# Two rows of activations as one 512-column operand in the SwiGLU output products and the mixer's output projection

## The chip, the cores and the metric

One core of a Trainium2 chip runs the whole program as one launch. The metric is the device time of that launch in microseconds (us), the median of the runs shown; less is better. PE is TensorE's matmuls, PEld its weight loads, DVE VectorE, ACT ScalarE, POOL GpSimd, SP the queue that issues the DMAs.

## The reference, cut to what matters

A two-layer encoder trunk over 256 positions of 1024 channels. Each layer has three sub-layers: a SwiGLU block, three token mixers with a merged output projection, and a second SwiGLU block; each ends in a residual and a LayerNorm:

```python
def swiglu(h, wi, wo):
    gu = h @ wi                                   # (256, 1024) @ (1024, 5632)
    return (jax.nn.silu(gu[..., :D_FF]) * gu[..., D_FF:]) @ wo   # (256, 2816) @ (2816, 1024)
...
x = layer_norm(ALPHA * x + 0.5 * mod[:, :, 2] * swiglu(h, ...), ln_w[l, 0], ln_b[l, 0])
...
x = layer_norm(ALPHA * x + mod[:, :, 5] * (merged @ w_out), ln_w[l, 1], ln_b[l, 1])
```

All of it is float32. The modulation `mod` is a product of the condition vector with a large matrix (`ada_w`), different for each sub-layer.

## The kernel before

Activations stand transposed: 128 channels on the partitions, 256 positions along a row, so a 1024-channel activation is 8 tiles of 128x256 and the 2816-channel one of a SwiGLU block is 22. A weight block is 128x128 and is the stationary operand; a product of one output tile m accumulates over its k blocks in one PSUM bank.

To keep float32's precision with the one-pass type float32r, most products are taken in three parts. `unit` (L321) loads up to 1024 columns of weights by one DMA into `raw` (4 buffers) and splits them in pieces of 512 columns, four k blocks each: `whi` is ACT's rounded copy, `wlo` DVE's remainder (5 buffers each). Activations are split in the same way by `split` (L308): `hhi`/`hlo` for the modulated input (`h_split`, L450), `ahi`/`alo` for the SwiGLU's product (L658 to 661), `hhi`/`hlo` again for the merged mixer output (L1364 to 1367). `mm3` (L341) then issues three matmuls per k block, of 128x128 weights by 256 columns each: `whi` by the high part, `whi` by the low part, `wlo` by the high part. All three add into the same 256 columns of a bank (`dense`, L349; `dbank`, L255, takes the first 256 of a bank's 512 columns, with 4 buffers). The mixers' input projections use `plain` float32 weights and an unsplit `h` instead (`h_split` with plain=True).

A SwiGLU block (`ffn`, L624) has two stages. In the first, 22 pairs of output tiles run over 8 k blocks. In the second (L663 to 669), 8 output tiles m run over 22 k blocks in three units of 8, 8 and 6; these are the second SwiGLU products. `side_work` (L373) puts pieces of the modulation (`ada`, L416: a DMA of 512 KB and a 1.22 us pass on DVE each) between the units. After each m, `ln_put` (L536) takes the bank: one DVE pass makes the residual `r = psum * gate + xa` (L541), then ACT squares it, DVE adds it into two running sums, and ACT (and DVE) prepare it as operand of the first products of the next sub-layer. For m = 0 a small matmul makes a mean that is taken off first. After m = 7 four matmuls make the LayerNorm's statistics; `early` (L510) issues the first four products of the next sub-layer, so that PE has work while `ln_end` (L570) finishes the norm.

The mixers end (L1432 to 1440) in the output projection: 8 output tiles over 8 k blocks with `wout`, each again followed by `ln_put`.

The order of instructions within an engine is laid by the Tile framework's scheduler, which may interleave what the source has one after the other; each engine then works its own list in order and waits on semaphores.

Of the kernel before, what the change touches and what calls it, by code (L numbers as in the profile page):

```python
# [10 lines left out]
F32R = mybir.dt.float32r  # L14
AF = mybir.ActivationFunctionType
# [4 lines left out]
MUL, ADD, SUB, MAX, MIN = ALU.mult, ALU.add, ALU.subtract, ALU.max, ALU.min  # L20

D, L, DEPTH, FF = 1024, 256, 2, 2816
NT, NF = D // 128, FF // 128
# [188 lines left out]
class Builder:  # L212
# [136 lines left out]
    def dense(self, out, w, x, off=0, k0=0, nk=8, first=True, last=True):  # L349
        for k in range(nk):  # L350
            self.product(out, w, off + k * 128, x[k0 + k], first and k == 0, last and k == nk - 1)

    def product(self, out, w, off, x, first, last, cols=128):
        if isinstance(w, list):
            self.mm3(out, w, off, x, first, last)
        else:
            self.mm(out, w[:, off:off + cols], x, first, last)
# [90 lines left out]


    def h_split(self, m, src, a, b, on_act=False, plain=False):  # L450
        h = self.t("hhi", 256, 8) if plain else self.t("hf", 256, 2)
        if on_act:
            x = self.act(h[:], src, AF.Identity, scale=a, bias=b)
        else:
            x = self.ts(h[:], src, a, MUL, b, ADD)
        if plain:
            self.h[m] = h[:]
            return x, x, x
        hi = self.t("hhi", 256, 8, F32R)
        lo = self.t("hlo", 256, 8, F32R)  # L460
        self.h[m] = (hi[:], lo[:])
        return (x, *self.split(hi[:], lo[:], h[:]))

    def start(self):
        x = self.x0 = self.lt("xa", (8, 256))
# [67 lines left out]
            self.ready[key] = y, wab[:, 1:2]  # L533
        self.adv = []

    def ln_put(self, m, psum):  # L536
        l, sub = self.lsub
        mod = self.mods[(l, sub)]
        r, xa = self.r, self.xa
        assert (l, sub, 2) in self.done  # L540
        self.stt(r[:, m, :], psum, mod[:, 16 + m:17 + m], xa[:, m, :], MUL, ADD)  # L541
        if m == 0:
            pb = self.bank("s", 2)
            self.mm(pb[:, 0:256], self.ones, r[:, 0, :], True, True)
            sm = self.sm = self.lt("lsm")
            self.act(sm[:], pb[:, 0:256], AF.Copy, scale=1.0 / 128)

            self.tt(xa[:, 1, :], xa[:, 1, :], sm[:], SUB)
            self.tt(r[:, 0, :], r[:, 0, :], sm[:], SUB)
            self.s1, self.s2 = self.lt("racc"), self.lt("lsa")  # L550
            self.act(self.s2[:], r[:, 0, :], AF.Square)
            self.u_put(0)
            return
        sq = self.lt("lsq", bufs=2)
        self.act(sq[:], r[:, m, :], AF.Square)
        if m < 7:
            x = self.tt(self.s1[:], r[:, 0, :] if m == 1 else self.s1[:], r[:, m, :], ADD)
            self.after(self.tt(xa[:, m + 1, :], xa[:, m + 1, :], self.sm[:], SUB), x)
            self.tt(self.s2[:], self.s2[:], sq[:], ADD)
        self.u_put(m)  # L560
        if m == 6:
            self.act(self.warm[:], sq[:, 0:1], AF.Ln, bias=1.0)
            self.p1, self.p2 = self.bank("s", 2), self.bank("s", 2)
            self.mm(self.p1[:, 0:256], self.onesd[:], self.s1[:], True, False)
            self.mm(self.p2[:, 0:256], self.onesd[:], self.s2[:], True, False)
        if m == 7:
            self.mm(self.p1[:, 0:256], self.onesd[:], r[:, m, :], False, True)
            self.mm(self.p2[:, 0:256], self.onesd[:], sq[:], False, True)
# [55 lines left out]
    def ffn(self, l, i):  # L624
        sub = 2 * i
        ap = self.ap
        acts = []
# [4 lines left out]
        for j in range(NF):  # L632
            ps, ws = [], []
            for q in (0, 1):
# [3 lines left out]
                else:  # L638
                    w = self.unit(u)
# [13 lines left out]
            pr = self.pt("ada_raw", 1024, 3)[:, 0:256]  # L653
            if ws or not pair:
                self.tt(pr, sg[:], pu, MUL)
            else:
                self.stt(pr, pu, bu, sg[:], ADD, MUL)
            hi = self.pt("ahi", 256, NF, F32R)  # L658
            lo = self.pt("alo", 256, NF, F32R)
            self.split(hi[:], lo[:], pr)  # L660
            acts.append((hi[:], lo[:]))
        self.ln_begin(l, sub)
        for m in range(8):  # L663
            pd = self.dbank()
            for k0, nk in ((0, 8), (8, 8), (16, 6)):
                self.side_work(m == (0 if own else SIDEM) and k0 == 0)
                w = self.unit(ap["wo"][l, i, m, :, k0:k0 + nk, :].rearrange("p k c -> p (k c)"), nk * 128)
                self.dense(pd, w, acts, 0, k0, nk, k0 == 0, k0 == 16)
            self.ln_put(m, pd)
        if sub == 0:  # L670
            self.early(self.mix_units(l)[:NE], NE)
        elif l + 1 < DEPTH:
# [676 lines left out]
    def merge(self, l, br, ys, first, last):  # L1349
        mg = self.mg  # L1350
        for m in range(8):
            gs = self.pt("gi", 256, 3)
            self.dma(gs[:], self.gd[br][:, m, :])
            if m % 2 == 0:
                w = self.unit(self.ap["pab"][l, br, m // 2].rearrange("p m k c -> p (m k c)"))
# [5 lines left out]
                self.stt(gs[:], gs[:], 1.0, pp, ADD, MUL)  # L1361
                self.tt(mg[:, m, :], mg[:, m, :], gs[:], ADD)
            if last:
                hi = self.t("hhi", 256, 8, F32R)  # L1364
                lo = self.t("hlo", 256, 8, F32R)
                self.split(hi[:], lo[:], mg[:, m, :])
                self.mh.append((hi[:], lo[:]))

    def mixers(self, l):
        A = self.A  # L1370
# [24 lines left out]
        with self.phase("w") as self.wp, self.phase("l") as self.lp:  # L1395
# [36 lines left out]
            self.relief = REL[5]  # L1432
            for m in range(8):
                w = ws[m] if m < NPRE else self.unit(wout[m])
                pd = self.dbank()
                self.dense(pd, w, self.mh)
                self.ln_put(m, pd)
            self.early(self.ffn_units(l, 1)[:NE], NPRE)
            self.relief = 0
            self.ln_end()  # L1440
# [53 lines left out]
```

## Time and profile before

| | before |
|---|---|
| median of 3 runs (lowest to highest) | 1677.54 us (1676.74 to 1681.32) |
| the profiled execution's own time | 1676.47 us |
| its span in the trace | 1674.7 us |
| PE busy, weight loads busy | 1583.2 us (95%), 1432.8 us (86%) |
| DVE, ACT, POOL busy | 1154.3, 804.9, 274.4 us |
| moved by DMA | 355.75 MB, mean 212 GB/s |

How to read it: matmuls are pipelined, so a record's duration (some 280 ns for a 256-column float32r matmul) is longer than the distance at which the next one starts; the distance is found by dividing a stretch by the matmuls in it. A weight load has a record of its own (LDWEIGHTS). "f32" in a shape also stands for float32r operands of PE.

### The profile page before, as it was taken

Reading aid. Unit: us, or ns where it says so; the run is one execution under the profiler, and the core shown is the slowest. Engines: PE = TensorE matmul, PEld = TensorE weight load, DVE = VectorE, ACT = ScalarE, POOL = GpSimd, SP = SyncE. Lnnn points to the kernel's source line nnn. Section 1 sums busy time; section 2 is a strip of 40 time slices with the busy share of each in tenths; the row PEclk is TensorE's granted clock in tenths of the full one; section 3 lists DMA queues with packets and bytes.
Section 4 is the critical chain, followed back from the end, with each engine's and each line's share of the span. In section 5 each row is a group of like instructions: output and inputs, shape, how many; then the busy total and the mean of one; then the engine's idle time right before and its main releaser. Section 6 shows DMA issues by size and latency. Waiting matters only on the chain.

```text
span 1674.7 us, 31925 instructions
## 1 busy us (share of the span) xinstructions
PE 1583.2 (95%) x12118; PEld 1432.8 (86%) x12118; DVE 1154.3 (69%) x2326; ACT 804.9 (48%) x1566; POOL 274.4 (16%) x376
## 2 busy tenths in 40 slices
PE   5999999979999989899999999999899998989996
PEld 2999998858787778899999999887678786989996
DVE  6788856375446778888888887465744557886665
ACT  2655545233243445655575555443323434565554
POOL 0000013292601001200030000345460000030001
PEclk9999999999999999999999999999899999999998
DMA  9898834635567554788769886346366654566662
GB/s 376 307 321 277 284 123 153 154 105 145 177 166 271 202 190 157 291 303 299 257 229 366 304 306 203 117 123 175 107 165 165 217 199 154 187 205 228 219 181 87
DMA packets 157881, 355.75 MB, mean 212 GB/s; under 512 B 55901, under 2 KB 75806, under 8 KB 157471
## 3 DMA queue, kind: packets, MB, share of 16 engines
q1 hardware_dynamic: 157726, 353.71, 64.3%
q8 instruction: 95, 1.56, 0.4%
q14 instruction: 60, 0.48, 0.1%
HBM read 332.11 MB, written 18.91 MB: 210 GB/s over the span
## 4 chain that ended last, share of the span: by engine, by line
PE 63%; DVE 6%; DMA 6%; POOL 4%; ACT 2%; issue 1%; SPq 1%; DVEq 0%; ACTq 0%; POOLq 0%
PE psd L293 53%; PE psm L293 6%; PE pss L293 4%; POOL arena L919 2%; DVE arena L290 2%; POOL arena L917 1%; DMA arena<-in_ada 1%; DVE arena L282 1%; DMA gi<-gate 1%; DVE wlo L309 1%; SPq L296 1%; DMA ada_raw<-in_ada 1%; DMA arena<-vrow 1%; ACT L279 1%; ACT arena L279 1%
## 5 line engine op out<-in xcount | busy, mean ns | idle before, releaser
L279 ACT ACTIVATE whi<-raw 128x512 fp32r<-128x512 f32 x608 | 370.7, 618 | 305.8 <-PE psd L293 253.2
L309 DVE TENSOR_TENSOR wlo<-raw,whi 128x512 fp32r<-128x512 f32 x608 | 405.5, 677 | 122.9 <-ACT whi L279 106.3
L293 PE MATMUL psd<-hhi,raw 128*128 128x256 f32 x1856 | 433.4, 388 | 1.5 <-DMA raw<-in_win 0.8
L293 PEld LDWEIGHTS psd<-hhi,raw 128*128 128x128 f32 x1856 | 346.8, 191 | 63.9 <-issue 10.4
L293 PE MATMUL psd<-hhi,whi 128*128 128x256 f32 x1360 | 383.0, 284 | 8.3 <-DVE r L290 4.6
L293 PE MATMUL psd<-hhi,wlo 128*128 128x256 f32 x1360 | 382.9, 283 | 1.9 <-DVE wlo L309 1.9
L293 PE MATMUL psd<-hlo,whi 128*128 128x256 f32 x1360 | 383.9, 283 | 0.0
L293 PEld LDWEIGHTS psd<-hhi,whi 128*128 128x128 f32 x1360 | 260.0, 192 | 9.5 <-ACT whi L279 5.1
L293 PEld LDWEIGHTS psd<-hhi,wlo 128*128 128x128 f32 x1360 | 260.2, 192 | 2.4 <-DVE wlo L309 2.3
L293 PEld LDWEIGHTS psd<-hlo,whi 128*128 128x128 f32 x1360 | 261.0, 192 | 0.1
L293 PE MATMUL psd<-alo,whi 128*128 128x256 f32 x704 | 198.7, 282 | 0.0
L581 POOL TENSOR_TENSOR r<-r,lmu 128x256 f32<-128x256 f32 x36 | 31.3, 901 | 1017.4 <-ACT lmu L279 1017.4
L293 PE MATMUL psd<-ahi,wlo 128*128 128x256 f32 x704 | 197.8, 281 | 0.0
L293 PE MATMUL psd<-ahi,whi 128*128 128x256 f32 x704 | 197.4, 280 | 0.0
L290 DVE SCALAR_TENSOR_TENSOR ada_raw<-ada_raw,cond 128x1024 f32<-128x1024 f32 x104 | 127.1, 1223 | 27.4 <-DMA ada_raw<-in_ada 27.0
L293 PEld LDWEIGHTS psd<-ahi,wlo 128*128 128x128 f32 x704 | 134.0, 190 | 0.3
L293 PEld LDWEIGHTS psd<-alo,whi 128*128 128x128 f32 x704 | 132.8, 189 | 0.2
L293 PEld LDWEIGHTS psd<-ahi,whi 128*128 128x128 f32 x704 | 132.2, 188 | 0.1
L279 ACT ACTIVATE arena<-arena 128x512 f32<-128x512 f32 (+4 forms) x108 | 65.5, 619 | 132.5 <-DVE arena L290 51.5
L293 PE MATMUL pss<-arena 128*64 128x128 f32 (+3 forms) x326 | 77.5, 387 | 18.7 <-ACT arena L279 8.6
L293 PE MATMUL psm<-arena 64*128 64x128 f32 (+6 forms) x824 | 80.3, 264 | 11.1 <-DVE arena L287 3.6
L917 POOL TENSOR_TENSOR arena<-arena 64x30 f32<-64x30 f32 (+14 forms) x120 | 67.9, 566 | 128.9 <-DMA arena<-zin 119.9
(223 smaller groups left out, 2164.6 us busy)
## 6 DMA issues: line engine op xcount, KB each, us to landing
raw<-in_wi SPq DMA_DIRECT2D x176, 512.0 KB, 4.7
raw<-in_win SPq DMA_DIRECT2D x118, 512.0 KB, 4.1
ada_raw<-in_ada SPq DMA_DIRECT2D x104, 512.0 KB, 5.7
raw<-in_wo SPq DMA_DIRECT2D x64, 512.0 KB, 4.2
arena<-in_ada SPq DMA_DIRECT2D x32, 512.0 KB, 4.8
raw<-in_wo SPq DMA_DIRECT2D x32, 384.0 KB, 3.6
raw<-in_pab SPq DMA_DIRECT2D x24, 512.0 KB, 3.5
raw<-in_wout SPq DMA_DIRECT2D x16, 512.0 KB, 4.4
```

Source lines behind the costliest of these rows:

```text
L279: return self.nc.scalar.activation(out=out, in_=in_, func=func, **k)
L282: return self.nc.vector.tensor_tensor(out=out, in0=a, in1=b, op=op)
L290: return self.nc.vector.scalar_tensor_tensor(out=out, in0=a, scalar=s, in1=b, op0=op0, op1=op1, **k)
L293: return self.nc.tensor.matmul(out, lhsT, rhs, start=start, stop=stop, **k)
L296: self.nc.sync.dma_start(out, in_)
L309: return self.act(hi, src, AF.Copy), (eng or self.nc.vector).tensor_tensor(out=lo, in0=src, in1=hi.bitcast(F32), op=SUB)
L581: x = sub_(out=r[:, m, :], in0=r[:, m, :], in1=mu[:], op=SUB)
L917: g.tensor_tensor(out=tv, in0=zw[:, j + 1:32, j:j + 1].to_broadcast([64, n, j]), in1=zw[:, j:j + 1, 0:j].to_broadcast([64, n, j]), op=MUL)
L919: g.tensor_tensor(out=zw[:, j + 1:32, 0:j], in0=zw[:, j + 1:32, 0:j], in1=tv, op=ADD)
```

## The change

The high and low parts of an activation are put side by side in one tile of 128x(2x256): `ax` for the SwiGLU's product and `hx` for `h` and the merged mixer output. A new `dense_wide` issues two matmuls per k block instead of three: `whi` by both parts as one operand of 512 columns, into the whole bank, and `wlo` by the high part into the first 256 columns. The bank's two halves are then added at the residual, by a second DVE pass in `ln_put`. The first SwiGLU products and the input projections keep their forms (`mm3` and plain), on the new tiles.

```diff
+    def dense_wide(self, out, w, x, k0=0, nk=8, first=True, last=True):
+
+        for k in range(nk):
+            (whi, wlo), x2 = w[k // 4], x[k0 + k]
+            off = k % 4 * 128
+            self.mm(out, whi[:, off:off + 128], x2.rearrange("p a b -> p (a b)"), first and k == 0, False)
+            self.mm(out[:, 0:256], wlo[:, off:off + 128], x2[:, 0, :], False, last and k == nk - 1)
...
     def h_split(self, m, src, a, b, on_act=False, plain=False):
-        h = self.t("hhi", 256, 8) if plain else self.t("hf", 256, 2)
+        h = self.t("hx", [2, 256], 8)[:, 0, :] if plain else self.t("hf", 256, 2)[:]
...
-        hi = self.t("hhi", 256, 8, F32R)
-        lo = self.t("hlo", 256, 8, F32R)
-        self.h[m] = (hi[:], lo[:])
-        return (x, *self.split(hi[:], lo[:], h[:]))
+        hx = self.t("hx", [2, 256], 8, F32R)
+        self.h[m] = (hx[:, 0, :], hx[:, 1, :])
+        return (x, *self.split(*self.h[m], h))
...
-    def ln_put(self, m, psum):
+    def ln_put(self, m, psum, wide=False):
...
-        self.stt(r[:, m, :], psum, mod[:, 16 + m:17 + m], xa[:, m, :], MUL, ADD)
+        self.stt(r[:, m, :], psum[:, 0:256], mod[:, 16 + m:17 + m], xa[:, m, :], MUL, ADD)
+        if wide:
+            self.stt(r[:, m, :], psum[:, 256:512], mod[:, 16 + m:17 + m], r[:, m, :], MUL, ADD)
...
-            hi = self.pt("ahi", 256, NF, F32R)
-            lo = self.pt("alo", 256, NF, F32R)
-            self.split(hi[:], lo[:], pr)
-            acts.append((hi[:], lo[:]))
+            ax = self.pt("ax", [2, 256], NF, F32R)
+            self.split(ax[:, 0, :], ax[:, 1, :], pr)
+            acts.append(ax)
...
-            pd = self.dbank()
+            pd = self.bank("d", 4)
...
-                self.dense(pd, w, acts, 0, k0, nk, k0 == 0, k0 == 16)
-            self.ln_put(m, pd)
+                self.dense_wide(pd, w, acts, k0, nk, k0 == 0, k0 == 16)
+            self.ln_put(m, pd, True)
...
-                hi = self.t("hhi", 256, 8, F32R)
-                lo = self.t("hlo", 256, 8, F32R)
-                self.split(hi[:], lo[:], mg[:, m, :])
-                self.mh.append((hi[:], lo[:]))
+                hx = self.t("hx", [2, 256], 8, F32R)
+                self.split(hx[:, 0, :], hx[:, 1, :], mg[:, m, :])
+                self.mh.append(hx)
...
-                pd = self.dbank()
-                self.dense(pd, w, self.mh)
-                self.ln_put(m, pd)
+                pd = self.bank("d", 4)
+                self.dense_wide(pd, w, self.mh)
+                self.ln_put(m, pd, True)
```

## Rows read from the trace of the kernel before

**Rows 1.** The page: span, busy time of the engines, shares of the chain that ended last.
```profile
span 1674.7 us, 31925 instructions
PE 1583.2 (95%) x12118; PEld 1432.8 (86%) x12118; DVE 1154.3 (69%) x2326; ACT 804.9 (48%) x1566; POOL 274.4 (16%) x376
...
PE 63%; DVE 6%; DMA 6%; POOL 4%; ACT 2%; issue 1%; SPq 1%; DVEq 0%; ACTq 0%; POOLq 0%
```

**Rows 2.** Groups of PE instructions by shape: count | busy us, mean ns of one | idle before.
```profile
L293 PE MATMUL psd<-hhi,raw 128*128 128x256 f32 x1824 | 425.9, 388 | 1.5 <-DMA raw<-in_win 0.8 <-DVE arena L290 0.5 <-PE psm L293 0.2
...
L293 PE MATMUL psd<-hhi,whi 128*128 128x256 f32 x1360 | 383.0, 284 | 8.3 <-DVE r L290 4.6 <-ACT sg L279 3.7
...
L293 PE MATMUL psd<-ahi,whi 128*128 128x256 f32 x704 | 197.4, 280 | 0.0
...
L293 PE MATMUL pss<-arena 128*128 128x512 f32 x64 | 32.4, 643 | 0.3 <-DVE arena L282 0.3
...
L293 PE MATMUL psm<-cst,arena 128*128 128x2 f32 x32 | 3.7, 246 | 0.0
```

**Rows 3.** Windows, busy us of each engine (count), clock, DMA: second products (two), first products.
```profile
988.00:996.00 8.00, 8.00 (x73) 8.00 (x73) 7.50 (x15) 4.25 (x8) 0.00 (x0) 1.00 0.87 287
1015.00:1045.00 30.00, 30.00 (x257) 30.00 (x257) 19.87 (x40) 17.31 (x32) 0.00 (x0) 1.00 0.67 197
900.00:960.00 60.00, 60.00 (x503) 60.00 (x502) 52.44 (x103) 32.62 (x64) 0.00 (x0) 1.00 0.91 309
```

**Rows 4.** The chain that ended last, a piece (start us, us, what) of second products.
```profile
999.08 47.47 PE psd L293 x403
```

**Rows 5.** Timeline of PE and its loads (start us, us, what) in a second-product stage.
```profile
994.98 0.28 PE L293 MATMUL psd<-ahi,whi 128*128 128x256 f32 x1
994.98 0.19 PEld L293 LDWEIGHTS psd<-alo,whi 128*128 128x128 f32 x1
...
995.09 0.28 PE L293 MATMUL psd<-alo,whi 128*128 128x256 f32 x1
```

**Rows 6.** Timeline of PE: 2-column, 512-column and 256-column plain float32 matmuls, merged.
```profile
30.74 1.84 PE L293 MATMUL psm<-cst,arena 128*128 128x2 f32 x16
...
33.56 3.70 PE L293 MATMUL pss<-arena 128*128 128x512 f32 x8
...
284.08 13.22 PE L293 MATMUL psd<-hhi,raw 128*128 128x256 f32 x60
```

**Rows 7.** Tile ahi on PE, 980 to 1052 us: count, ns min/median/max, first and last start.
```profile
L293 PE MATMUL psd<-ahi,whi x176: 276/281/286, 987.5 to 1050.2; 128*128 128x256 f32 x176
```

**Rows 8.** DVE instructions on the tile r: count, duration ns min/median/max, first and last start.
```profile
L290 DVE SCALAR_TENSOR_TENSOR r<-psd,mod,xa x48: 476/479/484, 182.6 to 1659.5; 128x256 f32<-128x256 f32 x48
```

**Rows 9.** Timeline of DVE in the third SwiGLU block's second products, tile m = 2.
```profile
1004.71 1.29 DVE L309 TENSOR_TENSOR wlo<-raw,whi 128x512 fp32r<-128x512 f32 x2
1005.92 0.48 DVE L290 SCALAR_TENSOR_TENSOR r<-psd,mod,xa 128x256 f32<-128x256 f32 x1
1006.32 0.68 DVE L309 TENSOR_TENSOR wlo<-raw,whi 128x512 fp32r<-128x512 f32 x1
```

**Rows 10.** Windows at both layers' output projections: PE, PEld, DVE, ACT, POOL, clock, DMA.
```profile
640.00:663.00 23.00, 19.13 (x153) 18.39 (x151) 21.48 (x49) 14.55 (x31) 0.00 (x0) 1.00 0.52 170
1446.00:1466.00 20.00, 18.12 (x145) 17.55 (x144) 19.28 (x46) 13.46 (x28) 0.00 (x0) 1.00 0.59 186
```

**Rows 11.** Groups of DVE instructions in layer 0's output projection, 640.6 to 662.3 us.
```profile
L290 DVE SCALAR_TENSOR_TENSOR r<-psd,mod,xa 128x256 f32<-128x256 f32 x7 | 3.4, 480 | 0.0
```

**Rows 12.** Who PE waited for: us in total, times, longest.
```profile
PE psd L293 <- DVE r L290: 5.1, 4, 2.5
```

**Rows 13.** Timeline at the second SwiGLU block's end: DVE's residual m = 7, PE's statistics.
```profile
857.52 0.48 DVE L290 SCALAR_TENSOR_TENSOR r<-psd,mod,xa 128x256 f32<-128x256 f32 x1
...
859.69 0.59 PE L293 MATMUL pss<-r,onesd 128*128 128x256 f32 x2
```

**Rows 14.** Timeline at the program's end.
```profile
1660.05 0.42 ACT L279 ACTIVATE lsq<-r 128x256 f32<-128x256 f32 x1 [5.87 <-DVE r L290]
```

More of the change, by code (lines that the diff above doesn't have):

```diff
@@ L450, in h_split @@
     def h_split(self, m, src, a, b, on_act=False, plain=False):
-        h = self.t("hhi", 256, 8) if plain else self.t("hf", 256, 2)
+        h = self.t("hx", [2, 256], 8)[:, 0, :] if plain else self.t("hf", 256, 2)[:]
         if on_act:
-            x = self.act(h[:], src, AF.Identity, scale=a, bias=b)
+            x = self.act(h, src, AF.Identity, scale=a, bias=b)
         else:
-            x = self.ts(h[:], src, a, MUL, b, ADD)
+            x = self.ts(h, src, a, MUL, b, ADD)
         if plain:
-            self.h[m] = h[:]
+            self.h[m] = h
             return x, x, x
-        hi = self.t("hhi", 256, 8, F32R)
-        lo = self.t("hlo", 256, 8, F32R)
-        self.h[m] = (hi[:], lo[:])
-        return (x, *self.split(hi[:], lo[:], h[:]))
+        hx = self.t("hx", [2, 256], 8, F32R)
+        self.h[m] = (hx[:, 0, :], hx[:, 1, :])
+        return (x, *self.split(*self.h[m], h))
     def start(self):
```

## The prediction

> **What bounds the kernel now.** I read the page first, then groups of PE instructions by shape, then windows over single stages, and last the timeline around single instructions. The page [rows 1] shows PE busy for 95% of the span and 63% of the chain that ended last; DVE, at 69%, holds 6% of that chain. So a change of PE's work should show, wherever PE is what ends last.
>
> The touched matmuls of the second SwiGLU products are three groups of 704, without idle time before them; one of the three stands in [rows 2]. What one costs is the distance to the next. A window counts whatever overlaps it, so I divide its length plus one duration (0.28 us) by its count [rows 3]: 8.28 us / 73 = 113.4 ns early in such a stage, 30.28 / 257 = 117.8 ns later, and 60.28 / 503 = 119.8 ns in the first products. The chain's piece of 403 matmuls says the same, 47.47 / 403 = 117.8 ns [rows 4]. The granted clock there is 1.00, the 2.4 GHz level, at which 256 columns at one per cycle take 106.7 ns; so a matmul costs 7 to 13 ns more than its columns.
>
> What the rest is, the loads tell. A weight load starts together with the matmul before it, and the matmul that uses it follows 0.11 us later [rows 5]. Matmuls of only 2 columns, each with a 128x128 load, still follow at (1.84 - 0.25) / 15 = 106 ns [rows 2, 6]: that is the load alone. A plain float32 matmul of 256 columns takes (13.22 - 0.39) / 59 = 217 ns and one of 512 takes (3.70 - 0.64) / 7 = 437 ns [rows 2, 6], with a load each: twice 109 and four times 109 ns, so where the columns last longer than a load, the load is hidden and a pass of 256 columns costs 109. In the touched products a load (106) and its cover (107) are equally long, and the handing over shows. I read it so: there the load sets the pace.
>
> **The change part by part.** *Matmuls.* Per k block it replaces three loads and three 256-column matmuls by two loads, a matmul of 512 and one of 256. The columns stay 768; one load in three goes. Before, a block costs 3 x 113.4 = 340 ns or 3 x 117.8 = 353 ns. After: the wide one hides the load of `wlo`, 217 ns (two passes of 109, as plain float32's 256); the narrow one must cover the wide one's load and stays at 113.4 to 117.8, of which I take the middle, 115.6. Sum 333. A SwiGLU block has 8 x 22 = 176 k blocks; about 32 run at the first pace (a stage starts at 987.5 [rows 7], and the piece at the second pace at 999.08 [rows 4], after the mean's matmuls of m = 0: some 11.1 us / 0.340), and 144 at the second: 32 x 340 + 144 x 353.4 = 61.8 us before, 176 x 333 = 58.6 after, a gain of 3.15. Four blocks: **-12.6 us**. No row has a float32r matmul of 512 columns, so bounds: with every load hidden a block costs 3 x 109 = 326 ns, which gives -17.3 us; if the wide one takes two narrow slots, 0. I stay near the first end because the 512-column float32 row costs no more than two of 256.
>
> *Are the weights ready sooner?* In the third SwiGLU block DVE is full in the first three tiles. The piece of `wlo` for the ninth k block of m = 2 is done at about 1005.4 (the first of two that end at 1006.0) [rows 9]; PE needs it 52 blocks after the stage's start at 987.5 [rows 7], with 32 blocks at 340 ns, 0.5 us for the mean's matmuls and 20 at 353 at about 1006.0 to 1006.1. So there are 0.6 to 0.7 us of slack. PE would come 0.7 us earlier, and DVE 0.4 later for one added pass: a stall of about **+0.5 us**, once. The other blocks have more slack or less side work; nothing there, and if that cover is gone, as much each, 1.5 in all.
>
> *The added DVE pass.* There are 48 passes `r<-psd,mod,xa` of 479 ns [rows 8], and the change adds as many; in a full stream the next instruction starts 0.40 us after one starts (1005.92 to 1006.32, [rows 9]). In the four SwiGLU stages DVE has room: 19.87 us busy in 30 of PE [rows 3]. A bank is held 0.4 us longer, of four banks at 7 us a tile. Nothing.
>
> In the output projections it is otherwise. From 640 to 663 DVE is busy 21.48 of 23 us and PE 19.13, in layer 1 19.28 of 20 and 18.12 [rows 10]. Seven of the eight residual passes lie there without any idle time before them [rows 11], and PE waits for them to free its banks, 5.1 us in total [rows 12]. What is queued behind the added pass is the same DVE list: splits, running sums, the next residual. So 7 x 0.40 = 2.8 us a layer, **+5.5 us** for two with rounding. Bounds: 0, if the scheduler moves splits out of this stretch, to 8 x 0.48 x 2 = 7.7. The shorter matmuls give nothing back here, since PE waits; if DVE had room, 2 x 64 blocks at 3 x 119.8 - 333 = 26 ns, 3.4 us.
>
> *After m = 7.* The statistics wait for the second pass. In the second SwiGLU block the residual starts at 857.52 and PE comes to its statistics at 859.69 [rows 13]: squaring ends near 858.5, so 1.1 us of slack hide one pass; the early products are the cover. At the program's end there are none: the squaring waits for the residual alone [rows 14], so one dependent pass, **+0.5 us**.
>
> *Operands and moves.* The wide matmul waits for `lo` as well as `hi`; before, `lo` was wanted 0.11 us after `hi`. For a SwiGLU block the last activation is wanted at the 22nd k block, so 21 blocks hide it; in the projection at most 0.4 us a layer, within the bound. No DMA, split or queue changes: the same loads, and tiles of the same size in all.
>
> **Sum:** -12.6 + 0.5 + 5.5 + 0.5 = -6.1 us. The profiled execution took 1676.47 us, its span plus 1.8; it becomes 1670.4. The median shown is 1.07 us above that execution, so **1671.4 us**. About 0.3%, 5.0 us, is what a measurement of this kernel can tell from no change: the bounds are 1672.5 and 1682.6.
>
> **The rivals.** *The cost is per matmul, not per load.* The 5 to 9 ns over 109 may be paid by each matmul, hidden load or not. Then a block saves one such fee: (32 x 4.6 + 144 x 9.0) x 4 = 5.8 us, against 6.5 of added cost: +0.7, 1678.2 us, no change. For it: the paces differ by operands, not by loads. Against it: plain float32 pays it not, with a load each. The Trainium skill has a rule that goes this way ("TensorE: Matmul & The Clock Gate", Back-to-back issue gap): a warm matmul of N columns takes N / 2.4 + 2.5 ns. By it a block would go from 327.5 to 325 ns and the change would save 704 x 2.5 ns = 1.8 us, an estimate from that page, and end at 1682.2. The trace does not agree where it matters here: 113.4 to 119.8 ns against the rule's 109.2.
>
> *The wide matmul takes two narrow slots* (slower). Place: the 704 wide matmuls; price: 235.6 ns instead of 217, a block stays as it was, and the 6.5 us of DVE are left: 1684.0 us. It decides from 226 ns on (6.1 us / 704 = 8.7 ns over 217): from there the kernel gains nothing. For it: no row shows this form. Against it: the 512-column float32 row.
>
> *The new place of `h` changes the pace of the first products.* At the same weights they run at 119.8 ns with `hhi` and 113.4 with `ahi` [rows 3], so something in the operands, perhaps where they lie, sets the pace. `hx` lies elsewhere. If these fell to 113.4: some 3740 matmuls (three groups of 1360 [rows 2], less the projections') x 6.4 ns = -24 us, 1647.4. Nothing else speaks for it.
>
> **How the numbers follow.** Forecast 0.66, fee per matmul 0.17, two slots 0.10, pace of `h` 0.07. The forecast's own range: -17.3 with the projections hidden and 1.0 left gives 1661; a narrow pace of 119.8 and 7.7 of DVE give 1676.2. Reaching over the fee's two values and not to the two others, which leaves out no more than 0.2, the range is 1661 to 1681. Faster: 0.74 of the forecast, all of the last case, a little of the fee, 0.58. Same: 0.16 of the forecast, 0.13 of the fee, 0.03 of the slots, 0.32. Slower: 0.10, mostly the slots.
>
> **What would show it.** Wide matmuls followed after 217 ns and narrow ones after 113 to 118; a SwiGLU's second products in about 59 us plus the statistics; `r` passes 96 instead of 48; DVE fuller and LayerNorm later by 2 to 3 us after each output projection; 0.5 us more at the end. It is wrong if the wide distance is 226 or more, if the first products' 119.8 moves, or if the projections take no longer.

## The result: slower by 1.0%, outside the predicted range

The changed kernel takes 1696.05 us (median of 4 runs, 1694.15 to 1696.68) where the kernel before takes 1677.44 (1676.74 to 1681.32) on the same chip: a ratio of 1.010, 95% interval 1.0077 to 1.0123. Forecast were 1671.4 us and a range of 1661 to 1681, so the sign was wrong too. The profiled execution took 1695.88 us; its span is 19.4 us longer than that of [rows 1].

The page of the kernel after: span, busy times, shares of the chain that ended last.

```profile
span 1694.1 us, 30315 instructions
PE 1592.3 (94%) x11286; PEld 1401.7 (83%) x11286; DVE 1171.5 (69%) x2374; ACT 807.8 (48%) x1566; POOL 274.2 (16%) x376
...
PE 63%; DVE 7%; DMA 6%; POOL 4%; ACT 3%; issue 2%; SPq 1%; ACTq 0%; DVEq 0%; POOLq 0%
```

There are 832 loads and matmuls fewer than in [rows 1], yet PE is busy 9 us longer and the span is longer by twice that.

**The second products.** Windows of the kernel after: two in a SwiGLU block's second products, one in the first products (busy us of PE, PEld, DVE, ACT and POOL with counts, granted clock, DMA's share, GB/s).

```profile
995.00:1008.00 13.00, 13.00 (x76) 11.29 (x75) 11.82 (x23) 5.84 (x11) 0.00 (x0) 1.00 0.99 358
1012.00:1042.00 30.00, 30.00 (x172) 26.08 (x171) 22.45 (x47) 17.01 (x33) 0.00 (x0) 1.00 0.65 190
1520.00:1580.00 60.00, 60.00 (x503) 60.00 (x502) 41.90 (x74) 32.70 (x63) 0.00 (x0) 1.00 0.72 230
```

Two matmuls make a k block now. Length plus the mean duration of one (0.34 us), over the count, times two: 13.34 / 76 x 2 = 351 ns early in the stage and 30.34 / 172 x 2 = 353 ns later, where [rows 3] gave 340 and 353 (one matmul more or less in the first window is 5 ns). The load engine is idle for an eighth of the time (26.08 of 30), so the loads really went, and nothing came of it. How the 353 ns are split, PE's timeline of the kernel after shows:

```profile
1000.16 0.40 PE L294 MATMUL psd<-ax,whi 128*128 128x512 f32 x1
1000.39 0.28 PE L294 MATMUL psd<-ax,wlo 128*128 128x256 f32 x1
1000.51 0.40 PE L294 MATMUL psd<-ax,whi 128*128 128x512 f32 x1
1000.75 0.28 PE L294 MATMUL psd<-ax,wlo 128*128 128x256 f32 x1
```

From a wide one to the narrow one 0.23 to 0.24 us, from there to the next wide one 0.12: the wide matmul takes two narrow slots, not the 217 ns of the forecast. The stage that ran from 987.48 to 1050.71 us (63.2) now runs from 994.51 to 1058.13 (63.6): 0.4 us lost instead of 3.15 gained, because its first 32 blocks had run at 340 ns. The first products stay at 60.28 / 503 = 119.8 ns, so `hx` changed nothing there.

**The residual.** Its passes, count and duration (ns min/median/max), and the program's end in the kernel after:

```profile
L291 DVE SCALAR_TENSOR_TENSOR r<-psd,mod,xa x48: 474/477/486, 181.7 to 1679.0; 128x256 f32<-128x256 f32 x48
L291 DVE SCALAR_TENSOR_TENSOR r<-psd,mod,r x48: 473/477/485, 182.7 to 1679.5; 128x256 f32<-128x256 f32 x48
```
```profile
1679.03 0.48 DVE L291 SCALAR_TENSOR_TENSOR r<-psd,mod,xa 128x256 f32<-128x256 f32 x1 [5.32 <-PE psd L294]
1679.54 0.48 DVE L291 SCALAR_TENSOR_TENSOR r<-psd,mod,r 128x256 f32<-128x256 f32 x1
1680.06 0.42 ACT L280 ACTIVATE lsq<-r 128x256 f32<-128x256 f32 x1 [5.72 <-DVE r L291]
```

Twice 48 passes, as forecast, and at the end 0.5 us from one pass to the next, as forecast.

**The output projections.** Windows from the last merge matmul to the first one of the next SwiGLU block, first the kernel before, then the kernel after, each with layer 0 and layer 1:

```profile
625.50:672.40 46.90, 37.71 (x298) 36.59 (x298) 37.73 (x82) 26.97 (x59) 6.33 (x7) 1.00 0.51 167
1431.90:1475.50 43.60, 37.66 (x299) 36.65 (x298) 36.23 (x80) 26.32 (x59) 6.30 (x7) 1.00 0.50 163
```
```profile
624.50:677.80 53.30, 41.64 (x235) 36.40 (x235) 41.30 (x91) 27.76 (x59) 5.97 (x7) 0.90 0.46 144
1446.30:1495.20 48.90, 39.47 (x235) 34.47 (x234) 39.27 (x87) 27.26 (x58) 5.90 (x7) 0.97 0.46 144
```

They are 6.4 and 5.3 us longer, 11.7 together. Length less PE's busy time is its idle time: 9.2 to 11.7 us and 5.9 to 9.4, 6.0 more. Of these, 2.3 lie at the ends, where PE waits for the norm's first operand, 3.9 us in each layer instead of 2.7. The other 5.7 us are PE's own, with fewer matmuls: 37.7 to 41.6 and to 39.5. The clock column (the share of TensorE's full clock that was granted) says why: 1.00 before, 0.90 and 0.97 after. The place of it in layer 0:

```profile
636.00:641.00 5.00, 1.31 (x8) 0.89 (x6) 2.05 (x5) 2.14 (x4) 0.00 (x0) 0.85 0.71 249
641.00:645.00 4.00, 3.88 (x11) 3.31 (x12) 3.74 (x8) 1.33 (x4) 0.00 (x0) 0.50 0.42 116
645.00:650.00 5.00, 2.69 (x11) 2.08 (x11) 3.44 (x8) 2.48 (x6) 0.00 (x0) 0.84 0.69 222
650.00:655.00 5.00, 5.00 (x21) 4.29 (x21) 4.83 (x12) 2.27 (x6) 0.00 (x0) 0.68 0.14 33
```

PE is nearly idle from 637 to 641, then works at 0.50 (the 1.2 GHz level), gets the full clock back, waits once more and falls again. Busy time by what is missing of the clock: 1.31 x 0.15 + 3.88 x 0.50 + 2.69 x 0.16 + 5.00 x 0.32 = 4.2 us, about the 3.9 that PE is busy longer. Whom PE waited for there (us, times, longest), and DVE's timeline around the longest wait:

```profile
PE pss L294 <- DVE r L291: 3.8, 1, 3.8
PE psd L294 <- DVE r L291: 3.1, 2, 2.3
```
```profile
636.29 0.48 DVE L291 SCALAR_TENSOR_TENSOR r<-psd,mod,xa 128x256 f32<-128x256 f32 x1 [1.15 <-PE psd L294]
639.43 1.23 DVE L291 SCALAR_TENSOR_TENSOR ada_raw<-ada_raw,cond 128x1024 f32<-128x1024 f32 x1 [2.66 <-DMA ada_raw<-in_ada]
...
640.59 0.48 DVE L291 SCALAR_TENSOR_TENSOR r<-psd,mod,r 128x256 f32<-128x256 f32 x1
```

The two passes of m = 0 are not neighbours in DVE's list: a modulation pass of the next block stands between them and waits 2.66 us for its transfer, and PE waits with it. In layer 1 no such pass stands there; a residual makes PE wait 3.7 us, behind splits of weights, among them those of the early products. PE's waits for residuals in the two projections come to 11.8 us, where [rows 12] has 5.1.

**The end of the second SwiGLU block.** From the last matmul of the second products to the first one of the next block, first in the kernel before, then in the kernel after, there with DVE's residual passes of m = 7:

```profile
856.55 0.28 PE L293 MATMUL psd<-ahi,wlo 128*128 128x256 f32 x1
868.83 0.28 PE L293 MATMUL psm<-hhi,whi 128*128 128x256 f32 x1
```
```profile
860.70 0.28 PE L294 MATMUL psd<-ax,wlo 128*128 128x256 f32 x1
863.56 0.48 DVE L291 SCALAR_TENSOR_TENSOR r<-psd,mod,xa 128x256 f32<-128x256 f32 x1
863.95 1.28 DVE L310 TENSOR_TENSOR wlo<-raw,whi 128x512 fp32r<-128x512 f32 x2
865.15 0.47 DVE L291 SCALAR_TENSOR_TENSOR r<-psd,mod,r 128x256 f32<-128x256 f32 x1
874.71 0.85 PE L294 MATMUL psm<-hx,whi 128*128 128x256 f32 x3 [1.62 <-ACT hx L280]
```

It takes 14.0 us instead of 12.3. The second pass stands behind two more splits, and the early products no longer cover the norm: PE waits 1.62 us. This is the added pass: the ten kernels with one pass in the SwiGLU blocks (before, e1, e3, e6, e9, e10, e11, e12, e14, e16) take 12.3 us here, the seven with two (after, e2, e4, e7, e8, e13, e15) 13.1 to 14.5. The same stretch behind the first and the third SwiGLU block takes 14.9 us in all of them, so there the pass is hidden.

**The sum.** Of the 19.4 us, 1.6 are the four SwiGLU stages (0.4 each), 1.7 the end of the second block, 11.7 the projections, 0.5 the program's end. Some 3.9 are left, in stretches that the change doesn't touch (below).

### The profile page after: what moved, and what is told of

Read it like the earlier page. It is cut to its first block, busy times and chain, and to the rows that moved or that the text cites. A ratio compares the mean times of both kernels' runs of the same rounds, so it can differ in the third digit from the quotient of the medians.

```text
span 1694.1 us, 30315 instructions
## 1 busy us (share of the span) xinstructions
PE 1592.3 (94%) x11286; PEld 1401.7 (83%) x11286; DVE 1171.5 (69%) x2374; ACT 807.8 (48%) x1566; POOL 274.2 (16%) x376
## 4 chain that ended last, share of the span: by engine, by line
PE 63%; DVE 7%; DMA 6%; POOL 4%; ACT 3%; issue 2%; SPq 1%; ACTq 0%; DVEq 0%; POOLq 0%
PE psd L294 53%; PE psm L294 5%; PE pss L294 3%; DVE arena L291 2%; POOL arena L926 2%; POOL arena L928 2%; DMA arena<-in_ada 1%; DVE arena L283 1%; ACT L280 1%; DMA raw<-in_win 1%; DMA raw<-in_wi 1%; DVE wlo L310 1%; SPq L297 1%; DMA gi<-gate 1%; ACT arena L280 1%
## 5 line engine op out<-in xcount | busy, mean ns | idle before, releaser
L294 PE MATMUL psd<-hx,whi 128*128 128x256 f32 (+1 forms) x2608 | 498.2, 290 | 10.3 <-DVE r L291 6.5
L294 PE MATMUL psd<-hx,raw 128*128 128x256 f32 x1856 | 432.5, 387 | 4.8 <-DMA raw<-in_win 3.9
L294 PEld LDWEIGHTS psd<-hx,whi 128*128 128x128 f32 x2608 | 413.8, 193 | 18.1 <-issue 7.3
L294 PEld LDWEIGHTS psd<-hx,raw 128*128 128x128 f32 x1856 | 345.8, 191 | 67.3 <-issue 10.3
L294 PE MATMUL psd<-hx,wlo 128*128 128x256 f32 x1360 | 385.6, 285 | 0.0
L294 PEld LDWEIGHTS psd<-hx,wlo 128*128 128x128 f32 x1360 | 263.2, 194 | 0.2
L294 PE MATMUL psd<-ax,whi 128*128 128x512 f32 x704 | 250.1, 399 | 0.0
L294 PE MATMUL psd<-ax,wlo 128*128 128x256 f32 x704 | 198.5, 283 | 0.0
L294 PEld LDWEIGHTS psd<-ax,whi 128*128 128x128 f32 x704 | 132.2, 188 | 31.8
L294 PEld LDWEIGHTS psd<-ax,wlo 128*128 128x128 f32 x704 | 132.2, 188 | 0.5
L294 PE MATMUL psm<-arena 64*128 64x128 f32 (+6 forms) x824 | 79.9, 263 | 13.1 <-DVE arena L288 4.1
```

What stands on the lines that cost most here:

```text
L294: return self.nc.tensor.matmul(out, lhsT, rhs, start=start, stop=stop, **k)
```

## The experiments

Every ratio is to the kernel before in the same runs on the same chip. "Projections" is the sum of two windows like those above, from each run's own profile.

**1. One part at a time.** Four kernels split the change. e1 keeps the new tiles, with the three matmuls and the one pass of before:

```diff
+            self.mm(out[:, 0:256], whi[:, off:off + 128], x2[:, 0, :], first and k == 0, False)
+            self.mm(out[:, 0:256], whi[:, off:off + 128], x2[:, 1, :], False, False)
             self.mm(out[:, 0:256], wlo[:, off:off + 128], x2[:, 0, :], False, last and k == nk - 1)
```

> The tiles of the change (both parts side by side) with the matmuls and the single residual pass of before. Columns theory (a float32r matmul costs some 118 ns for every 256 columns, whatever load stands beside it, and the loss comes from the added DVE passes and from the DVE list around them): as before, 1675 to 1680 us, and paces of 113, 118 and 120 ns as before. Layout theory (the new places of the tiles in memory cost the time): 1688 us or more, and no stretch at 113 ns in the second SwiGLU products.

e2 and e3 have that form in one place and the wide one, with both passes, in the other:

```diff
-                self.dense_wide(pd, w, self.mh)
-                self.ln_put(m, pd, True)
+                self.dense_one(pd, w, self.mh)
+                self.ln_put(m, pd)
```

> The change in the second SwiGLU products alone. Columns theory: a block of three passes stays at 353 ns, each of the four stages 0.4 us longer, and what the added pass does at the boundary between two SwiGLU blocks (4.4 us in the changed kernel): 1679 to 1686 us, the output projections as before. Rival (the wide matmuls themselves cost the time, 704 of the 832 being here): 1692 us or more.

> The change in the output projections alone. Columns theory: the added residual passes on a full DVE and their places in its list make both projections later, 4 to 9 us each: 1686 to 1693 us. Rival (the wide matmuls themselves; only 128 of 832 are here): 1680 us or less.

e4 keeps both passes and goes back to narrow matmuls, one into each half of the bank, in all but the first k block of a tile:

```diff
-            self.mm(out, whi[:, off:off + 128], x2.rearrange("p a b -> p (a b)"), first and k == 0, False)
+            if first and k == 0:
+                self.mm(out, whi[:, off:off + 128], x2.rearrange("p a b -> p (a b)"), True, False)
+            else:
+                self.mm(out[:, 0:256], whi[:, off:off + 128], x2[:, 0, :], False, False)
+                self.mm(out[:, 256:512], whi[:, off:off + 128], x2[:, 1, :], False, False)
```

> The changed kernel with two narrow matmuls, one into each half of the bank, for each wide one except the first of a tile; the second residual pass stays. Columns theory: nothing is gained by the wide form, so the time stays that of the changed kernel, 1693 to 1699 us, with a load more per block at the same 353 ns. Rival (the wide form costs the time): 1677 to 1683 us. Load theory (my forecast's): 20 ns a block more than the changed kernel, some 12 us above it.

And e10 is e3 without the second pass, so that the product of the weights' high part with the activations' low part is left out of the sum:

```diff
-                self.ln_put(m, pd, True)
+                self.ln_put(m, pd)
```

> The change in the output projections alone, and there without the second residual pass: the product of the weights' high part with the activations' low part is computed by the wide matmuls and left out of the sum. Pass theory (what made the projections later is the added work on a full DVE): as before, 1672 to 1679 us, each projection within 1 us of the kernel before. Rival (the wide matmul itself, with its wait for the low part and its bank): 1684 us or more, as with the pass.

| kernel | us (before: 1675.1, for e10 1678.0) | ratio, 95% interval | projections, us |
|---|---|---|---|
| e1, tiles alone | 1674.6 | 0.9995 (0.9971 to 1.0019) | 89.8 |
| e2, SwiGLU alone | 1676.9 | 0.9995 (0.9973 to 1.0017) | 92.5 |
| e3, projections alone | 1688.7 | 1.0081 (1.0058 to 1.0105) | 99.1 |
| e10, the same without the second pass | 1683.5 | 1.0043 (1.0023 to 1.0063) | 92.6 |
| e4, second pass without the wide form | 1684.6 | 1.0050 (1.0026 to 1.0073) | 95.7 |
| the whole change | 1696.05 (1677.44) | 1.0100 (1.0077 to 1.0123) | 102.2 |

The layout costs nothing; that theory falls. The SwiGLU part, 704 of 832 wide matmuls, makes no difference that can be measured (the time came out 2 us under what either theory expected, and the 4.4 us that its expectation puts at the boundary of two SwiGLU blocks are 1.7 by the rows above): the rival that blames the wide matmul itself falls. The projections, with 128 of the wide matmuls, carry the loss, within the 1686 to 1693 us expected. What there belongs to the pass and what to the wide form is less clear. Against 90.5 us in the profile of before, both together make the projections 8.6 us longer (e3), the pass alone 5.2 (e4), the wide form alone 2.1 (e10); but e2, whose projections are those of before, is 2.0 off as well, so only the pass shows. The times of e4 and e10 lie between the theories: e4 8 us under the lowest of the columns theory and 2 over the rival's highest, e10 4.5 over the highest of the pass theory and just under its rival's 1684, though its projections are 0.9 and 1.2 us off those of before, where 1 was expected. Both lost the rest elsewhere (the point on the stretches that the change doesn't touch, in the next section).

That narrow matmuls with three loads keep the pace in e4 speaks against my load theory, which wanted 20 ns a block more than the changed kernel. The window of e4's second products:

```profile
195.00:232.00 37.00, 37.00 (x314) 36.79 (x314) 27.39 (x58) 20.98 (x40) 0.00 (x0) 1.00 0.63 192
```

The first block of each tile still has a wide matmul; five of them lie in this window and count for two. 37.28 / 319 x 3 = 351 ns a block, with a load more.

**2. Is it the columns?** e5 leaves out the matmul by `wlo`, so that only wide ones with one load each are left:

```diff
-            self.mm(out[:, 0:256], wlo[:, off:off + 128], x2[:, 0, :], False, last and k == nk - 1)
```

> The changed kernel without the narrow matmul of each k block: the product of the weights' low part with the activations' high part is left out in the second SwiGLU products and in the output projections, so that every matmul of those stages is a wide one with one load. Columns theory (the pace belongs to the columns): the next wide one starts after 235 ns, a stage of 176 blocks takes about 42 us. Load theory (a load that has to be covered sets the pace; a wide one hides it): 217 ns and about 39 us.

PE's timeline of e5, the first wide matmuls of the first block's second products, merged:

```profile
175.82 4.36 PE L294 MATMUL psd<-ax,whi 128*128 128x512 f32 x18
```

(4.36 - 0.39) / 17 = 233.5 ns, and a stage of 44.2 us with a few waits for splits in it (the three others take 41.7 to 48.7; 1637.7 us in all, one run). At 217 ns it would have been 38 us. A load twice as well covered changed the distance by 2 ns: the extra is paid by the column, about 10 ns for every 256, whether one load stands beside 512 of them or two (e4).

**3. What sets the pace of the columns?** The rival on `h` in the prediction had noted that the same weights run at 113 ns with `ahi` and at 119.8 with `hhi`. By the addresses that the built programs give the tiles (no trace has them), `hhi`, `hlo`, `whi` and `wlo` of the kernel before all begin at a multiple of 128 bytes of their partition, `ahi`, `alo` and `yx` 64 bytes off one. `hx` again begins at a multiple, `ax` 64 off: the change moved neither against the weights. e6 and e7 move the weights, by 64 unused bytes ahead of them:

```diff
         self.act(x[:], x[:], AF.Copy, scale=ALPHA)
+        pad = self.t("pad", 16, 1)
+        self.nc.gpsimd.memset(pad[:], 0.0)
```

> The kernel before with 64 unused bytes per partition ahead of the weights' tiles, so that the weights' addresses are 64 off a multiple of 128 while h stays on one (the activations move along with the weights and stay apart from them). Address theory (the pace of a float32r matmul goes by where weights and moving operand lie against each other: 120 ns where both stand alike to 128 bytes, 113 where they don't): the first products go from 120 to 113.3 ns, some 3740 x 6.6 ns less, 1650 to 1657 us. Rival (the pace does not go by addresses): 120 ns, 1674 to 1680 us.

> The changed kernel with the same 64 bytes. Address theory: first products at 113.3 ns, 1669 to 1675 us, the second products still at 353 ns a block. Rival: 120 ns, 1693 to 1699 us.

e9 puts the 64 bytes at the start of the pool instead, ahead of `h` and of the weights, so that both move and stand alike again; e12 pads by 32 bytes where e6 does (`self.t("pad", 8, 1)`).

> The kernel before with the 64 unused bytes ahead of h as well, so that h and the weights both stand 64 off a multiple of 128 and alike again. Address theory (what counts is how the two stand against each other): 120 ns in the first products, 1672 to 1679 us. Rival (weights on a multiple of 128 are slow, or any shift would have done): 113 to 118 ns, 1650 to 1657 us.

> The kernel before with 32 unused bytes ahead of the weights instead of 64; h stands 32 bytes off from them, the activations still 64. If alike means equal to 128 or to 64 bytes: first products at 113 to 118 ns, about 1651 us. If the next 32 bytes make no difference: 120 ns, about 1674 us.

The same 60 us of first products in e6, in e9 and in e12:

```profile
900.00:960.00 60.00, 60.00 (x532) 60.00 (x531) 53.88 (x106) 34.52 (x66) 0.00 (x0) 1.00 0.89 315
```
```profile
900.00:960.00 60.00, 60.00 (x502) 60.00 (x501) 51.91 (x102) 32.89 (x65) 0.00 (x0) 1.00 0.89 314
```
```profile
900.00:960.00 60.00, 60.00 (x509) 60.00 (x508) 53.37 (x104) 33.61 (x66) 0.00 (x0) 1.00 0.89 317
```

60.28 over the count: 113.3, 120.1 and 118.4 ns. In these streams of narrow matmuls the pace is 120 where the two operands stand alike, and 113 or 118 where they don't. e6 takes 1651.4 us against 1673.0 (0.9872, 0.9850 to 0.9893): it beats both kernels with 64 bytes. e9 is the kernel before again (0.9990, 0.9971 to 1.0009), so it is not the shift as such. e7 takes 1666.9 (0.9973, 0.9952 to 0.9994), 2 us under what was expected: the change on top of the pad still costs 15 us, and its second products still take 353 ns a block. e12's single run, 1672.2 us beside 1678.0, fits the 118 of its row; neither of its two expectations, 113 to 118 ns with 1651 us and 120 ns with 1674, came out whole. Modulo 512 bytes, the length of a weight block's row, the distances run are 0, 32, 64 and (`ahi`) 192; that 128 is the period no run shows, nor what in the memory makes the difference. The wide form doesn't follow the rule: in the projections `hx` and the weights stand alike, and a block takes 353 ns in the changed kernel (six blocks from 655.17 us) and 347 in e3 (six from 652.89), where three narrow matmuls at 120 would be 360. There it gained 7 to 13 ns a block, with 128 blocks 1 to 2 us, an estimate, against the 8.6 us that e3's projections lost.

**4. 113 or 118?** In the kernel before, the pace falls from 113 to 118 ns at the first plain float32 matmul of a stage, the mean's. e11, on top of e6, makes that matmul float32r too:

```diff
-            self.mm(pb[:, 0:256], self.ones, r[:, 0, :], True, True)
+                on, rr = self.lt("onesr", 128, dt=F32R), self.lt("rr", dt=F32R)
+                self.act(on[:], self.ones, AF.Copy)
+                self.act(rr[:], r[:, 0, :], AF.Copy)
+                self.mm(pb[:, 0:256], on[:], rr[:], True, True)
```

> The padded kernel before, with the mean's matmul behind the first output tile of a SwiGLU block in float32r (its operands rounded by ACT) instead of plain float32. Phase theory (the plain matmul between the float32r ones throws the stream from the pace of 113 to the one of 118 ns): the second products stay at 113 ns, 4 x 430 x 4.5 ns = 7.7 us less than the padded kernel, 1641 to 1646 us. Rival (any matmul of another kind in between, or the place itself, does it): 118 ns, 1649 to 1654 us.

Windows of e11: second products of the first block, first products and second products of the third:

```profile
180.00:210.00 30.00, 30.00 (x267) 30.00 (x266) 23.60 (x50) 17.78 (x34) 0.00 (x0) 1.00 0.72 227
890.00:950.00 60.00, 60.00 (x512) 60.00 (x512) 53.08 (x104) 33.97 (x66) 0.00 (x0) 1.00 0.88 317
985.00:1015.00 30.00, 30.00 (x257) 30.00 (x256) 24.21 (x50) 17.51 (x35) 0.00 (x0) 1.00 0.72 227
```

113.4, 117.7 and 117.8 ns. In the first block the pace stayed at 113 behind the mean, as the phase theory has it; in the third even the first products, 113 in e6, ran at 118 from their start. In the fourth it fell at the mean, at 1586.8 us, although that was float32r:

```profile
1576.00:1586.00 10.00, 10.00 (x91) 10.00 (x89) 5.72 (x11) 5.05 (x11) 0.00 (x0) 1.00 0.63 180
1588.00:1612.00 24.00, 24.00 (x207) 24.00 (x205) 16.20 (x32) 12.24 (x23) 0.00 (x0) 1.00 0.62 183
```

113.0 and 117.3 ns. So the type of the mean's matmul doesn't decide it. 1656.0 us (0.9870, 0.9842 to 0.9898), no better than e6 and over both expectations. The pace has two values with the same operands, most stretches keep the one that they have (e4's second products change every few us), and what gives one or the other stays open.

**5. Why do the projections cost so much?** Three kernels each take away one suspect, two of them with a control. e8 keeps the modulation passes behind the second pass of m = 0 in DVE's list:

```diff
+            if m == 0:
+                self.hold = x
...
+            if self.hold:
+                self.after(x, self.hold)
```

> The changed kernel, with the modulation passes of the next block kept behind the second residual pass of m = 0 in DVE's list. List theory (a modulation pass that waits for its DMA stands between the two residual passes of m = 0 in layer 0, and the wait of 3.8 us on PE and the half clock after it follow from that): the wait falls under 1 us, the granted clock stays at 1.00 behind it, 1688 to 1692 us; layer 1 stays as it is. Rival (PE would wait there anyhow, for DVE's load): 1694 us or more.

1689.6 us (1.0110, 1.0087 to 1.0133): within the 1688 to 1692 of the list theory, but the kernel before took 1673.0 there, and the ratio is no better than the change's. The wait moved on: the modulation pass now stands ahead of the residual of m = 1, and PE waits longer than before for that.

```profile
PE psd L295 <- DVE r L292: 6.3, 2, 5.4
```

e13 moves every second split's subtraction in the projections to POOL, e14 does so in the kernel before:

```diff
-REL = (0, 0, 0, 0, 0, 0)
+REL = (0, 0, 0, 0, 0, 2)
```

> The changed kernel with every second subtraction of a weight split moved from DVE to the idle POOL while an output projection runs (11 of 512 columns a layer, 0.6 us each on DVE). Load theory (the projections are later because DVE has more to do there than PE has): PE's waits and the half clock behind them shrink, the two projections together 5 us or more shorter than in the changed kernel (102 us there), 1685 to 1691 us. Rival (what counts is where a residual pass stands in the list, or the wide matmul itself): the projections stay at 100 us or more, 1693 us or more.

> The same relief in the kernel before, as a control. Load theory: PE waits little for DVE there, so the two projections (90.5 us) become at most 3 us shorter, 1674 to 1678 us. Rival (DVE's load is not it): as before or longer, 1677 us or more.

The projections of e13, both layers:

```profile
621.00:671.50 50.50, 39.56 (x236) 34.42 (x235) 42.06 (x81) 27.52 (x60) 21.15 (x17) 0.97 0.49 152
1435.60:1483.80 48.20, 39.22 (x234) 34.36 (x234) 42.57 (x79) 27.46 (x60) 20.58 (x17) 0.96 0.47 148
```

DVE issues 8 to 10 instructions fewer in each, but is busy longer, 42.1 and 42.6 us instead of 41.3 and 39.3: while POOL works, some of the others take longer (in layer 0 the passes `xa<-xa,lsm` 571 ns on average instead of 418). PE is idle 10.9 and 9.0 us, little less than in the changed kernel. The 98.7 us lie between the two expectations; the time, 1687.9 us (1.0095, 1.0058 to 1.0131), does not differ measurably from the change's ratio. e14 gained nothing either (1.0021, 1.0004 to 1.0039). The edit did not lighten DVE, so whether DVE's load is the cause stays untested.

e15 keeps what waits for a transfer of the next block back: modulation passes and DVE's part of the early products' splits behind the residual of m = 1, ACT's part of them behind the mean's copy of m = 0. e16 is the same order in the kernel before:

```diff
+        if (sub, m) == (1, 1):
+            self.hold = (self.hold[0], x)
...
+            if self.fence:
+                for later, earlier in zip(parts_, self.fence):
+                    self.after(later, earlier)
```

> The changed kernel with everything of the next block that waits for its own transfer (the modulation passes, and the splits of the weights for the early products) kept behind the residual passes of m = 1 of the output projection in DVE's list, and behind the mean's copy in ACT's. List theory (a pass or split that waits for its DMA stands ahead of the residual passes that free PE's banks, PE starves and its clock falls): PE's longest waits for the residual, 3.8 and 3.7 us, fall under 2 us, the clock stays at 1.00 behind them, and the two projections together come to 97 us or less from 102; 1686 to 1692 us. Work theory (the added pass and the wide form take their time wherever they stand): 100 us or more, 1693 us or more.

> The same order in the kernel before, as a control: under either theory its projections (90.5 us) change by no more than 2 us, 1673 to 1679 us.

The projections of e15, and whom PE waited for in layer 0:

```profile
622.30:673.30 51.00, 40.90 (x235) 35.59 (x234) 41.58 (x90) 27.20 (x60) 6.28 (x7) 0.93 0.48 151
1440.30:1487.80 47.50, 37.83 (x235) 33.15 (x235) 39.68 (x89) 27.20 (x59) 5.98 (x7) 1.00 0.46 149
```
```profile
PE psd L295 <- DVE r L292: 2.9, 2, 2.2
PE psd L295 <- ACT whi L281: 2.6, 1, 2.6
```

The longest wait for a residual fell from 3.8 to 2.2 us in layer 0 and from 3.7 to 2.6 in layer 1, which kept its full clock; but ACT's splits, moved back, now make PE wait 2.6 us in layer 0, and the clock falls there all the same. 98.5 us and 1687.7 (1.0085, 1.0064 to 1.0105): of the 11.7 us the order gives back 3.7, a third, and less than the list theory wanted; e16 is the kernel before (1.0007, 0.9988 to 1.0026). No single place is the cause, as far as these kernels show: each wait taken away became another. Nor does a long wait need the added pass. In e2, with one pass in the projections and the time of the kernel before, PE waits 4.2 us in layer 0 behind a modulation pass that waits 2.63 us for its transfer, and in e9 3.5 us for an operand; the clock falls in both (0.93 and 0.96), and their layer 0 takes 49.1 and 47.3 us. So how much of the 11.7 us belongs to the pass, to the order of the list and to the one profiled execution stays open.

## Why the prediction was wrong

- **The step that failed first: "there the load sets the pace", and with it the 217 ns of the wide matmul, -12.6 us.** Taken from plain float32, where 512 columns cost no more than twice 256, it did not carry over to float32r. Its extra of 7 to 13 ns belongs to the columns: 235 ns for the wide one (353 a block), 233.5 with no other load in the stage (e5), no more with three loads (e4). The stages measured +1.6 us, so this step is 14.2 us of the miss. That the load alone takes 106 ns and the stage's columns 107 was a coincidence that I read as a cause. The Trainium skill's rule ("TensorE: Matmul & The Clock Gate", Back-to-back issue gap) would give the wide one 512 / 2.4 + 2.5 = 215.8 ns, an estimate from that page; the trace, with 235 ns, doesn't agree.
- **The rival that came true** was the wide matmul that takes two narrow slots: its price of 235.6 ns is what was measured, over its deciding point of 226. I gave it 0.10, held against it by a row of another data type. It said 1684.0; the rest of the miss is in the next three points.
- **The step that was mis-sized: the added DVE pass in the projections, +5.5 with a bound of 7.7.** Measured were 11.7 us. The part that I had priced, PE's waiting, came to 6.0; what I left out is that PE's clock falls behind a long wait: 5.7 us more busy time for fewer matmuls. The bound had no room for it. [rows 10] show 1.00 behind waits of up to 2.5 us, but the kernel before has the fall right behind these stretches, where PE waits 2.7 us for the norm; windows from there on:

```profile
669.70:680.00 10.30, 6.61 (x37) 6.00 (x36) 10.30 (x24) 8.04 (x20) 8.75 (x8) 0.83 0.55 179
1472.80:1482.00 9.20, 5.51 (x31) 5.12 (x30) 9.20 (x22) 6.62 (x17) 7.96 (x8) 0.81 0.57 182
```

The Trainium skill describes it ("TensorE: Matmul & The Clock Gate", HAM oscillation — how this bites in real kernels): behind a long wait the matmuls start at the lower clock, so that the wait is paid for again. The trace agrees, with 0.50 behind the wait of 3.8 us. The split into 6.0 and 5.7 is that of two executions: e1 and e9, which take the time of the kernel before, show 0.96 in layer 0 and are busy 77.1 and 77.3 us in both projections, where the kernel before is 75.4. I had also reckoned with a full DVE at a steady rate; what PE met was the order of the list.

- **The step put at nothing: "1.1 us of slack hide one pass" behind m = 7 of the second SwiGLU block.** It holds for the pass alone. In DVE's list two splits stand between the two passes, the statistics come later than the early products cover, and the block's end takes 1.7 us longer.
- **The stretches that the change doesn't touch: nothing forecast, some 3.9 us measured.** Layer 1's mixers and merges, from the end of the early products to the last merge matmul, took 366.4 us before and 373.5 after; other stretches gave some of these 7.1 back. Eight kernels with narrow matmuls and one pass everywhere (before, e1, e6, e9, e11, e12, e14, e16) took 364.5 to 367.8 there in their profiles, the nine others 367.2 to 373.5 (e5, which leaves matmuls out, 377.1). In e10 the order of the instructions on every engine is that of e1 in this stretch, and it took 371.3 against 364.8. Of these 6.5 us, 2.8 are one wait of PE for DVE (5.7 instead of 2.9), and 3.7 are busy time, at a granted clock of 0.97 instead of 0.99. Why DVE is later there stays open.
- **The rival on `h`** had the right premise, that a place in memory sets the pace, and the wrong consequence: `hx` stands against the weights as `hhi` did. Its price of 24 us is what 64 bytes give in e6 (21.6).
- **Right were** the 96 passes, the 0.5 us at the end, SwiGLU stages that hide their passes (but for the second block's end), and no gain or loss in waiting for `lo`. The stall of 0.5 us in the third block never came, since nothing ran ahead.

## What to carry to other kernels

A wider moving operand saves loads, and that is worth something only where loads set the pace: before counting on it, look at the same data type, and test with a kernel that has nothing but the wide form. Price a wait of PE twice, once for the idle time and once for the half clock behind it, and look at what else stands in the list of the engine that it waits for before adding a pass to it. Where one matmul shape shows two paces, compare the operands' addresses before changing the shape: 64 bytes of padding were worth 1.3% here, and the change -1.0%.

## What the runs showed of the hardware that was not expected

- The pace of a stream of 256-column float32r matmuls depends on how weights and moving operand stand in their partitions: 120 ns for each where both begin at the same offset to 128 bytes (0 and 0 in the kernel before, 64 and 64 in e9), 113.3 where they are 64 apart (e6, most of its first products), 118.4 where they are 32 apart (e12). Plain float32, with 217 ns in [rows 6] and operands alike, has no such extra: 108.5 a pass. The Trainium skill ("SBUF — State Buffer", A bandwidth-pool intuition that's wrong (but worth ruling out)) gives the weight load a read port independent of the moving operand's. One would conclude, though the Trainium skill does not say it, that their places don't matter to each other; in these runs they do.
- With operands 64 or 192 bytes apart there are two paces, 113 and 118 ns, which mostly last for tens of us (in e4 for a few); the wide matmuls followed after 233 to 235 ns on average.
- The granted clock fell to 0.50 behind a wait of 3.8 us in which PE had no work, came back after some 5 us of work, and fell again behind a wait of 2.3 us. A wait of 2.6 us in layer 1 of e15 left it at 1.00, so the length of a wait alone doesn't tell.
